# Twenty of the 22 up tiles of a transformer block's second FFN by Strassen's seven products, on one core of a Trainium2 chip

## The chip, the cores and the metric

The kernel runs as one program on one core of a Trainium2 chip. The metric is the device time of one execution in microseconds (us); several runs are compared by their median. A profiled execution gives the trace that all views below are read from.

The engines are named as in the profile: PE is TensorE's matmuls and PEld its weight loads, DVE is VectorE, ACT is ScalarE, POOL is GpSimd, SP is SyncE, whose queue issues transfers here. Each engine works through its own queue in order and waits on semaphores for the others.

## What is computed

Two layers on a sequence of 512 tokens of width 1024, with a context of 256 tokens: the first mixes by a Fourier and a Hyena branch, the second by multi-head latent attention, and each is followed by an FFN with a convolution over the tokens in its gate. The change is in the FFN of the second layer, which works on the 512 tokens alone:

```python
def _conv_ffn(h, w_up, conv_w, conv_b, w_down):
    gate, val = jnp.split(h @ w_up, 2, axis=-1)
    return (jax.nn.silu(_dwconv3(gate, conv_w, conv_b)) * val) @ w_down

def _dwconv3(x, w, b):
    xp = jnp.pad(x, ((0, 0), (1, 1), (0, 0)))
    return xp[:, :-2] * w[0] + xp[:, 1:-1] * w[1] + xp[:, 2:] * w[2] + b

# in reference(), per layer:
    x = x + g2 * _conv_ffn(_modulate(_rms_norm(x, norm2[i]), sh2, sc2), *ffn)
```

All arrays are float32. `w_up` is 1024 x 5632 (gate and value, 2816 each), `w_down` 2816 x 1024.

## The kernel before

Everything stands transposed: 128 features on the partitions, tokens along the free axis, so `x`, and the normalized input `h`, are 8 tiles of 128 x 512. A float32 product is made of three fast matmuls: each operand is split into a rounded high part (`hi`, an ACT copy) and the rest (`lo`, a DVE subtraction), and `mm3` adds high x high, high x low and low x high in PSUM. The three matmuls are lines 158, 159 and 160; the splits are lines 133 and 138, and the loads of raw weights line 146, in the profile.

The hidden width of 2816 is 22 tiles of 128 (`f`). `up(f)` loads two weight tiles of 128 x 1024 (gate and value), splits them, and multiplies each with the 8 tiles of `h` (`hh`, `hl`): 8 k x 2 x 3 = 48 matmuls of 512 columns, or twice as many of 256 for the first tile, which runs by token halves. The gate is convolved (`conv3`: ACT line 373, DVE lines 374 and 375), passed through Silu (line 1175), multiplied with the value (line 1177), and split for the next product. After 8, 16 and all 22 tiles `res_proj` multiplies them by `w_down` for each of 8 output tiles `m`, and line 1143 adds the result, times a gate, to `x`. The down part has 8 x 22 x 3 = 528 matmuls of 512 columns.

PSUM has three buffers of 1024 columns (`mm`) and two of 512 (`ms`); raw, high and low weights have three buffers each (`wr`, `wh`, `wl`, in pool `W`). Raw weights come on SP's queue in the order of their use, as buffers come free. In this part the order of work on the engines is left to the scheduler; in the mixer and the filter (`MIX_ORDER`, `FILTER_ORDER`) and in the attention (`ORDER`) it is written out by hand as a list of steps.

The second layer's `layer1` runs the attention, then the output projection `w_o` by token halves (256-column matmuls), with the norm of the FFN's input hooked in: per half, the squares are summed, `fin` makes the root, and `apply` makes `hh` and `hl` (lines 308, 309, 313). Then it calls `self.ffn(1, ...)`, and `build` writes `x` out.

## Time and profile before

| | |
|---|---|
| median of 3 runs | 1634.23 us |
| lowest, highest | 1628.58, 1636.04 us |
| profiled execution | span 1633.7 us, from its first to its last instruction |
| busy in the span: PE, DVE, ACT, POOL | 1590.5, 1047.7, 620.7, 109.5 us |
| transfers | 173.35 MB, mean 106 GB/s, all issued by SP but for 1.3 MB of instructions |

No other time is recorded for the profiled execution than its span. In the rows of the profile, `L158 PE MATMUL mm<-hh,wh 128*128 128x512` means line 158, the engine, the operation, the tile written and the tiles read, and the shape; then come the count, and behind a bar the busy time, the mean ns of one, and the idle time just before, with what ended it. A row of the timeline begins with the start and the duration in us; a row of the chain of waits gives start, time on the chain, and the step. Matmuls are pipelined, so their durations overlap, and their pace is read from start to start.

### The profile page before, as it was taken

How to read it: one execution, taken by the hardware profiler on the slowest of the kernel's cores; microseconds unless marked ns; L12 is line 12 of the kernel's file. 1: busy time of each engine (PE TensorE's matmuls, PEld its weight loads, DVE VectorE, ACT ScalarE, POOL GpSimd, SP SyncE). 2: the span in 40 equal slices, each digit the busy share in tenths (PEclk: the TensorE clock that was granted, in tenths of full speed). 3: DMA queues.
4: the chain of work that ended last, by engine and by line, in shares of the span. 5: the costliest groups of instructions: out<-in, count | busy, mean ns of one | idle time of the engine just before them, and what ended most of it. 6: DMA issues, size and time to landing. Idle time of an engine off the chain costs nothing.

```text
span 1633.7 us, 20802 instructions
## 1 busy us (share of the span) xinstructions
PE 1590.5 (97%) x8248; PEld 1300.4 (80%) x8248; DVE 1047.7 (64%) x1702; ACT 620.7 (38%) x883; POOL 109.5 (7%) x165
## 2 busy tenths in 40 slices
PE   7999998999999999999999989999999999999999
PEld 5787888888888888888888877666659888878887
DVE  6779869878785355643454665899987544344243
ACT  4441234333222113221033335988954432233131
POOL 0121134000000000000000000212210000000000
PEclk9999998999999999999999998999999999999999
DMA  9336402533443234432342220000024222232222
GB/s 361 109 105 231 156 29 78 192 118 112 159 155 117 77 129 145 164 104 77 113 160 86 83 70 1 13 11 14 0 99 147 78 103 92 90 104 90 90 91 90
DMA packets 54541, 173.35 MB, mean 106 GB/s; under 512 B 6187, under 2 KB 9453, under 8 KB 53421
## 3 DMA queue, kind: packets, MB, share of 16 engines
q1 hardware_dynamic: 54445, 172.03, 30.5%
q8 instruction: 65, 1.06, 0.2%
q14 instruction: 31, 0.25, 0.0%
HBM read 166.24 MB, written 5.77 MB: 105 GB/s over the span
## 4 chain that ended last, share of the span: by engine, by line
PE 81%; DVE 14%; issue 2%; ACT 1%; POOL 1%; DMA 1%; SPq 0%; POOLq 0%; DVEq 0%; ACTq 0%
PE mm L158 24%; PE mm L159 23%; PE mm L160 23%; PE pv L1611 2%; DVE wl L138 1%; DVE S L1587 1%; DVE junk L243 1%; PE s L1557 1%; DVE wr L1626 1%; PE k L158 1%; PE k L160 1%; PE k L159 1%; DVE hl L313 1%; PE mm L616 1%; DVE mx L1571 0%
## 5 line engine op out<-in xcount | busy, mean ns | idle before, releaser
L158 PE MATMUL mm<-hh,wh 128*128 128x512 f32 (+2 forms) x1360 | 481.7, 357 | 1.8 <-ACT wh L133 0.9
L159 PE MATMUL mm<-hl,wh 128*128 128x512 f32 (+2 forms) x1360 | 479.3, 353 | 2.3 <-DVE hl L313 2.3
L160 PE MATMUL mm<-hh,wl 128*128 128x512 f32 (+2 forms) x1360 | 478.7, 353 | 1.6 <-DVE wl L138 1.6
L133 ACT ACTIVATE wh<-wr 128x1024 fp32r<-128x1024 f32 (+1 forms) x192 | 197.8, 1033 | 571.1 <-PE mm L159 547.9
L138 DVE TENSOR_TENSOR wl<-wr,wh 128x1024 fp32r<-128x1024 f32 (+2 forms) x192 | 231.0, 1205 | 236.2 <-ACT wh L133 229.6
L158 PEld LDWEIGHTS mm<-hh,wh 128*128 128x128 f32 x1360 | 257.5, 190 | 48.7 <-issue 7.8
L159 PEld LDWEIGHTS mm<-hl,wh 128*128 128x128 f32 x1360 | 257.8, 190 | 39.0 <-DVE hl L313 3.5
L160 PEld LDWEIGHTS mm<-hh,wl 128*128 128x128 f32 x1360 | 257.6, 190 | 37.6 <-DVE wl L138 2.2
L243 DVE SCALAR_TENSOR_TENSOR junk<-wr,sb 128x1024 bf16<-128x1024 f32 x128 | 156.2, 1220 | 40.4 <-DMA wr<-wmodT 39.8
L158 PE MATMUL mm<-ah,wh 128*128 128x512 f32 (+1 forms) x480 | 172.4, 359 | 0.0
L160 PE MATMUL mm<-ah,wl 128*128 128x512 f32 (+1 forms) x480 | 172.2, 359 | 0.0
L159 PE MATMUL mm<-al,wh 128*128 128x512 f32 (+1 forms) x480 | 172.0, 359 | 0.0
L1143 DVE SCALAR_TENSOR_TENSOR xr<-mm,mod,xr 128x512 f32<-128x512 f32 (+1 forms) x100 | 61.7, 631 | 154.8 <-PE mm L160 153.1
L159 PEld LDWEIGHTS mm<-al,wh 128*128 128x128 f32 x480 | 90.5, 189 | 14.1 <-DVE al L138 0.2
L158 PEld LDWEIGHTS mm<-ah,wh 128*128 128x128 f32 x480 | 90.4, 188 | 14.2 <-issue 0.3
L160 PEld LDWEIGHTS mm<-ah,wl 128*128 128x128 f32 x480 | 90.4, 188 | 14.2
L1611 PE MATMUL pv<-S,V 128*128 128x512 f32 x192 | 93.9, 598 | 2.5 <-ACT S L1590 2.5
L1175 ACT ACTIVATE fg<-fg 128x772 f32<-128x772 f32 (+1 forms) x44 | 32.6, 741 | 97.7 <-DVE fg L375 90.9
L1565 ACT ACTIVATE S<-s,rks 128x512 f32<-128x512 f32 x96 | 62.6, 685 | 12.4 <-PE pv L1611 8.5
L1611 PEld LDWEIGHTS pv<-S,V 128*128 128x128 f32 x192 | 34.5, 190 | 34.7 <-issue 29.3
L1587 DVE TENSOR_TENSOR S<-S,mx 128x1536 f32<-128x1536 f32 x32 | 55.3, 1749 | 2.3 <-POOL mx L1583 2.3
L1583 POOL PARTITION_ALL_REDUCE mx<-mx x16 | 44.9, 2804 | 163.6 <-DVE mx L1580 163.6
(337 smaller groups left out, 2269.6 us busy)
## 6 DMA issues: line engine op xcount, KB each, us to landing
wr<-w_up SPq DMA_DIRECT2D x88, 512.0 KB, 3.2
wr<-wmodT SPq DMA_DIRECT2D x80, 512.0 KB, 3.2
wr<-w_dn SPq DMA_DIRECT2D x32, 512.0 KB, 3.3
wm<-wmod0a SPq DMA_DIRECT2D x8, 1024.0 KB, 9.2
wr<-w_in SPq DMA_DIRECT2D x16, 512.0 KB, 4.2
wr<-w_out SPq DMA_DIRECT2D x13, 512.0 KB, 3.3
wr<-w_dn SPq DMA_DIRECT2D x17, 384.0 KB, 3.0
wr<-w_o SPq DMA_DIRECT2D x11, 512.0 KB, 3.2
```

What stands on the lines that cost most here:

```text
L133: self.nc.scalar.activation(dst, src, AF.Copy)
L138: (eng or self.nc.vector).tensor_tensor(dst, src, hi.bitcast(F32), op=ALU.subtract)
L158: mmul(out, wh, xh, start=start, stop=False)
L159: mmul(out, wh, xl, start=False, stop=False)
L160: mmul(out, wl, xh, start=False, stop=stop)
L243: nc.vector.scalar_tensor_tensor(junk, raw, 1.0, self.sb[:, j, :], op0=ALU.mult, op1=ALU.mult, accum_out=acc)
L1143: nc.vector.scalar_tensor_tensor(x[m][:, a2:b2], ps[:, a2:b2], mod[:, 8 * sec + m, c : c + 1], x[m][:, a2:b2], op0=ALU.mult, op1=ALU.add)
L1175: nc.scalar.activation(g[:, :n], g[:, :n], AF.Silu)
L1565: nc.scalar.activation(c.S[a][j // 3][:, j % 3, :], c.ps[a, j], AF.Copy, scale=c.r[:, g : g + 1])
L1583: nc.gpsimd.partition_all_reduce(c.m[a][:, 1, :], c.m[a][:, 0, :], P, bass.bass_isa.ReduceOp.max)
L1587: v.tensor_tensor(c.S[a][h], c.S[a][h], mb.to_broadcast([P, 3, T]), op=ALU.subtract)
L1611: nc.tensor.matmul(c.P[a], V[:, j, o : o + 128], c.S[a][j // 3][:, j % 3, :], start=j == 0, stop=j == 5)
```

## The change

The second FFN gets its own function, `ffn_blocks`, with its order written out in `UP_ORDER`. Tiles 0 and 1 are made as before (step `U` for tile 1). For tiles 2 to 21 the product of the two weight tiles (gate and value, each with the two halves of the 1024 inputs) with `h` (two halves of the inputs by two halves of the tokens) is a 2 x 2 block product, and is made of seven block products, `P1` to `P7`, of 12 matmuls of 256 columns each:

- The four sums of blocks of `h` are formed once (`T`, in the `quarter` tiles) and split (`Th`, `Tl`). For that `norm` keeps its unrounded result (`whole`), with a further ACT pass.
- The four sums of weight blocks are formed per tile: two by transfers on POOL's queue, the second of each pair adding to what the first has landed (`S1`), two by DVE (`S2`, `S4`). `Hv`, `Hg`, `Ha`, `Hb` and `Lv`, `Lg`, `La`, `Lb` split the value's weights, half of the gate's, and the two tiles of sums. Only half of the gate's raw weights is loaded on SP (`Rg`), all of the value's (`Rv`).
- The blocks of the gate and the value are put together from PSUM by `K1` (ACT) and `C1`, `Ua`, `Xv`, `Ub`, `C2`, `C4`, `C3` (DVE). `Ca`, `Cb`, `Cc`, `Si`, `Ml`, `Ah`, `Al` are the convolution, Silu, the product and its split, as before.

The downs run in five groups of 5, 5, 4, 4 and 4 tiles (`UP_GROUPS`) instead of three, between the ups; `Rd`, `Hd`, `Ld` load and split their weights, `D` multiplies, `X` adds to `x`: 40 of each. In a step's name the numbers are the tile, or the group and the output tile. A list's order holds for PE, DVE, ACT, SP and POOL.

```diff
--- before.py
+++ after.py
@@ -81,6 +81,44 @@
+UP_ORDER = """
+S1.2 Rv2 Rv3 Rg2 S1.3 Hv2 S2.2 T1 Ha2 U1 Lv2 Ca0 Th1 La2 Hg2 Tl1 T3 S4.2 Th3 T2 Rv4 Hb2 Cb0 Th2 Tl3 Lb2 Tl2 S1.4 Cc0 P1.2 Ca1 T4 Si0 P2.2 Lg2 Th4 Ml0
+K1.2 S2.3 P5.2 Ah0 C1.2 Hv3 Tl4 P6.2 Lv3 P7.2 Ha3 Ua2 S4.3 Xv2 P1.3 Rg3 Ub2 La3 P4.2 Rv5 K1.3 C2.2 Cb1 P3.2 S2.4 Hg3 Cc1 Lg3 P2.3 Si1 C3.2 Hb3 Ml1 P5.3
...
+Lb5 Hv6 Hg5 P6.5 C1.5 S1.7 Ca4 Lv6 P7.5 Lg5 Ua5 S2.6 P1.6 Ub5 Ha6 Xv5 C2.5 P4.5 Ml3 K1.6 La6 Ah3 P3.5 S4.6 Cb4 Rg6 P2.6 Hb6 C3.5 Cc4 S2.7 Rd0.0 P5.6
+Si4 Lb6 Hv7 P6.6 Hg6 C1.6 S1.8 Lv7 P7.6 Ha7 Lg6 Ua6 C4.5 P1.7 Ub6 Xv6 C2.6 P4.6 La7 K1.7 Ml4 P3.6 S4.7 Ah4 Al3 Rg7 P2.7 Al4 Hb7 C4.6 C3.6 Rd0.1 Ca5
+P5.7 Lb7 Hd0.0 Hg7 C1.7 P6.7 S1.9 Ca6 Ld0.0 Lg7 Rd0.2 P7.7 Cb5 Hd0.1 Rv8 Ua7 Cc5 D0.0 Ub7 Si5 Xv7 C2.7 Ld0.1 S2.8 Rd0.3 Ml5 P4.7 S4.8 Ah5 X0.0 Cb6 P3.7
...
+Si21 X3.5 Hd4.0 Ml21 Ld4.0 Ah21 Rd4.3 Al21 D3.7 Hd4.1 X3.6 Ld4.1 Rd4.4 D4.0 Hd4.2 X3.7 Ld4.2 Rd4.5 D4.1 Hd4.3 X4.0 Ld4.3 Rd4.6 D4.2 Hd4.4 X4.1 Ld4.4
+Rd4.7 D4.3 Hd4.5 X4.2 Ld4.5 D4.4 Hd4.6 X4.3 Ld4.6 D4.5 Hd4.7 X4.4 Ld4.7 D4.6 X4.5 D4.7 X4.6 X4.7
+"""
+UP_GROUPS = ((0, 5), (5, 10), (10, 14), (14, 18), (18, 22))
+UP_WHOLE = 2
@@ -251,7 +289,7 @@
             self.nc.vector.scalar_tensor_tensor(self.A[i][k][:, j, a:b], sc, 1.0, self.pcol[:, o + a : o + b], op0=ALU.add, op1=ALU.mult)
 
 
-    def norm(self, i, k, x, hh, hl, c0, n, tp):
+    def norm(self, i, k, x, hh, hl, c0, n, tp, whole=None):
 
 
 
@@ -304,11 +342,18 @@
 
         def scaled(d):
             A, B = self.A[i][k][:, j, :], self.mod[i][:, 24 * k : 24 * k + 8, j]
+            if whole is not None:
+                u = box[d] = whole(d)
+                nc.vector.scalar_tensor_tensor(u, x[d][:, c0 : c0 + n], A[:, d : d + 1], box["R"][:, :n], op0=ALU.mult, op1=ALU.mult)
+                nc.scalar.activation(u, u, AF.Identity, bias=B[:, d : d + 1])
+                return nc.scalar.activation(hh[d][:, c0 : c0 + n], u, AF.Copy)
             u = box[d] = tp()
             nc.vector.scalar_tensor_tensor(u[:, :n], x[d][:, c0 : c0 + n], A[:, d : d + 1], box["R"][:, :n], op0=ALU.mult, op1=ALU.mult)
             return nc.scalar.activation(hh[d][:, c0 : c0 + n], u[:, :n], AF.Identity, bias=B[:, d : d + 1])
 
         def low(d):
+            if whole is not None:
+                return nc.vector.tensor_tensor(hl[d][:, c0 : c0 + n], box.pop(d), hh[d][:, c0 : c0 + n].bitcast(F32), op=ALU.subtract)
             B = self.mod[i][:, 24 * k : 24 * k + 8, j]
             return nc.vector.scalar_tensor_tensor(hl[d][:, c0 : c0 + n], box.pop(d)[:, :n], B[:, d : d + 1], hh[d][:, c0 : c0 + n].bitcast(F32),
                                                   op0=ALU.add, op1=ALU.subtract)
@@ -1715,7 +1760,7 @@
         nt = self.pool("nt", bufs=5)
         hp = self.pool("h2p")
         self.xp = self.pool("xres")
-        tp = lambda: self.t(nt, [P, 512], F32, "nt")
+        tp = lambda: self.t(nt, [P, 256], F32, "nt")
         x = [self.t(self.xp, [P, T], F32, f"xr{d}") for d in range(KD)]
         for d in range(KD):
             nc.sync.dma_start(x[d], xd[d])
@@ -1726,14 +1771,302 @@
         half = [[(0, 256)], [(256, 256)]]
         hh = [self.t(hp, [P, T], F32R, f"hh{d}") for d in range(KD)]
         hl = [self.t(hp, [P, T], F32R, f"hl{d}") for d in range(KD)]
-        hook, rest = self.norm_hook(*[self.norm(1, 1, x, hh, hl, c, 256, tp) for c in (0, 256)])
-        self.res_proj(1, 2, oh, ol, KD, lambda m: I["w_o"][m], x, half, hook, ready=2)
-        rest()
+        quarter = [[None] * 2 for _ in range(2)]
+        for a, b in ((0, 0), (0, 1), (1, 1), (1, 0)):
+            quarter[a][b] = self.t(self.xp, [P, 4, 256], F32, "quarter", 5)
+        whole = lambda b: lambda d: quarter[d // 4][b][:, d % 4, :]
+        hook, rest = self.norm_hook(*[self.norm(1, 1, x, hh, hl, 256 * b, 256, tp, whole(b)) for b in range(2)])
+        first = []
+
+        def whook(stage, j, m):
+            hook(stage, j, m)
+            if stage and j == 6:
+                first.extend(self.wload(I["w_up"][1, 0, q]) for q in range(2))
+
+        self.res_proj(1, 2, oh, ol, KD, lambda m: I["w_o"][m], x, half, whook, ready=2)
         self.close("pO")
         self.close("pa")
         self.dbg("xa1", x)
-        self.ffn(1, x, hh, hl, T, [(0, T)], half, None)
+        self.ffn_blocks(x, hh, hl, quarter, first, rest.steps)
         return x
+
+    def ffn_blocks(self, x, hh, hl, quarter, first, steps):
+
+        nc, I = self.nc, self.I
+        v = nc.vector
+        ENG = mybir.EngineType
+        take, f2, a2 = steps
+        i = 1
+        ap = self.pool("act1", bufs=9)
+        tm = self.pool("ftm1", bufs=2)
+        bl = self.pool("blk", bufs=2)
+        th = [self.t(bl, [P, 4, 256], F32R, f"th{q}", 1) for q in range(4)]
+        qf = lambda a, b: quarter[a][b].rearrange("p a b -> p (a b)")
+        tl = [None] * 4
+        form = {"1": (0, 0), "2": (1, 1), "3": (0, 1), "4": (1, 0)}
+        k_ = {}
+        acts = {}
+
+        def T_(n):
+            a, b, c, e = qf(0, 0), qf(0, 1), qf(1, 0), qf(1, 1)
+            if n == "1":
+                v.tensor_tensor(a, a, b, op=ALU.subtract)
+            elif n == "3":
+                v.tensor_tensor(b, e, b, op=ALU.subtract)
+            elif n == "2":
+                v.scalar_tensor_tensor(e, e, -1.0, a, op0=ALU.mult, op1=ALU.subtract)
+            else:
+                v.scalar_tensor_tensor(c, e, -1.0, c, op0=ALU.mult, op1=ALU.subtract)
+
+        def Th(n):
+            self.hi(th[int(n) - 1].rearrange("p a b -> p (a b)"), qf(*form[n]))
+
+        def Tl(n):
+            q = int(n) - 1
+            tl[q] = self.t(self.xp, [P, 4, 256], F32R, "quarter", 5)
+            self.lo(tl[q].rearrange("p a b -> p (a b)"), qf(*form[n]), th[q].rearrange("p a b -> p (a b)"))
+
+        def pair(n=1024):
+            return self.t(self.W, [P, 1024], F32R, "wh")[:, :n], self.t(self.W, [P, 1024], F32R, "wl")[:, :n]
+
+        def Rv(f):
+            k_["rv", f] = self.wraw(I["w_up"][i, f, 1])
+
+        def Rg(f):
+            k_["rg", f] = self.wraw(I["w_up"][i, f, 0]) if f < UP_WHOLE else self.wraw(I["w_up"][i, f, 0, :, 512:1024], 512)
+
+        def H(name, f, src, dst):
+            k_[name, f] = dst
+            self.hi(dst[0], src)
+
+        def L(name, f, src):
+            self.lo(k_[name, f][1], src, k_[name, f][0])
+
+        def Hv(f):
+            H("wv", f, k_["rv", f], pair())
+
+        def Lv(f):
+            L("wv", f, k_["rv", f])
+
+        def Hg(f):
+            if f < UP_WHOLE:
+                k_["wg", f] = [[self.t(ap, [P, T], F32R, f"a{q}") for q in "hl"] for _ in range(2)]
+                for b in range(2):
+                    self.hi(k_["wg", f][b][0], k_["rg", f][:, 512 * b : 512 * b + 512])
+            else:
+                H("wg", f, k_["rg", f][:, 0:512], [self.t(bl, [P, 512], F32R, f"wg{q}", 1) for q in "hl"])
+
+        def Lg(f):
+            if f < UP_WHOLE:
+                for b in range(2):
+                    self.lo(k_["wg", f][b][1], k_["rg", f][:, 512 * b : 512 * b + 512], k_["wg", f][b][0])
+            else:
+                L("wg", f, k_["rg", f][:, 0:512])
+
+        def S1(f):
+            s = k_["sa", f], k_["sb", f] = [self.t(bl, [P, 1024], F32, "sum", 4) for _ in range(2)]
+            g, u = I["w_up"][i, f, 0], I["w_up"][i, f, 1]
+            for t_ in s:
+                nc.gpsimd.dma_start(t_[:, 512:1024], g[:, 0:512])
+            for t_, src in zip(s, (g[:, 512:1024], u[:, 0:512])):
+                nc.gpsimd.dma_start(t_[:, 512:1024], src, accum_op=ALU.add)
+
+        def S2(f):
+            s = k_["sa", f]
+            v.tensor_tensor(s[:, 0:512], s[:, 512:1024], k_["rv", f][:, 0:512], op=ALU.add)
+
+        def S4(f):
+            v.tensor_tensor(k_["sb", f][:, 0:512], k_["sa", f][:, 0:512], k_["rv", f][:, 512:1024], op=ALU.add)
+
+        def Ha(f):
+            H("wa", f, k_["sa", f], pair())
+
+        def La(f):
+            L("wa", f, k_["sa", f])
+
+        def Hb(f):
+            H("wb", f, k_["sb", f], pair())
+
+        def Lb(f):
+            L("wb", f, k_["sb", f])
+
+        def prod(ps, w, o, mov):
+            for q in range(4):
+                s = slice(o + 128 * q, o + 128 * q + 128)
+                self.mm3(ps, w[0][:, s], w[1][:, s], *mov(q), q == 0, q == 3)
+
+        part = lambda a, b: lambda q: (hh[4 * a + q][:, 256 * b : 256 * b + 256], hl[4 * a + q][:, 256 * b : 256 * b + 256])
+        tf = lambda n: lambda q: (th[n - 1][:, q, :], tl[n - 1][:, q, :])
+
+        def P1(f):
+            m = k_["m", f] = self.mm()
+            prod(m[:, 0:256], k_["wv", f], 0, part(0, 0))
+
+        def P2(f):
+            prod(k_["m", f][:, 512:768], k_["wv", f], 512, part(1, 0))
+
+        def P5(f):
+            b = k_["b", f] = self.ms()
+            prod(b[:, 0:256], k_["wa", f], 512, tf(1))
+
+        def P6(f):
+            prod(k_["m", f][:, 0:256], k_["wa", f], 0, tf(2))
+
+        def P7(f):
+            prod(k_["m", f][:, 512:768], k_["wb", f], 512, tf(3))
+
+        def P4(f):
+            prod(k_["m", f][:, 0:256], k_["wg", f], 0, tf(4))
+
+        def P3(f):
+            prod(k_["b", f][:, 0:256], k_["wb", f], 0, part(1, 1))
+
+        def K1(f):
+            k_["t", f] = self.t(bl, [P, 3, 256], F32, "t")
+            nc.scalar.copy(k_["t", f][:, 0, :], k_["m", f][:, 0:256])
+
+        def plus(out, a, b):
+            v.tensor_tensor(out, a, b, op=ALU.add)
+
+        def minus(out, a, b):
+            v.scalar_tensor_tensor(out, a, -1.0, b, op0=ALU.mult, op1=ALU.subtract)
+
+        def C1(f):
+            k_["v", f] = self.t(tm, [P, T], F32, "fv", 3)
+            plus(k_["v", f][:, 0:256], k_["t", f][:, 0, :], k_["m", f][:, 512:768])
+
+        def Ua(f):
+            plus(k_["t", f][:, 1, :], k_["t", f][:, 0, :], k_["m", f][:, 0:256])
+
+        def Ub(f):
+            plus(k_["t", f][:, 2, :], k_["t", f][:, 1, :], k_["m", f][:, 512:768])
+
+        def Xv(f):
+            plus(k_["v", f][:, 256:512], k_["t", f][:, 1, :], k_["b", f][:, 0:256])
+
+        def C2(f):
+            k_["g", f] = self.t(tm, [P, T], F32, "fg")
+            minus(k_["g", f][:, 256:512], k_["t", f][:, 2, :], k_["b", f][:, 0:256])
+
+        def C4(f):
+            minus(k_["g", f][:, 0:256], k_["t", f][:, 2, :], k_["m", f][:, 0:256])
+
+        def C3(f):
+            plus(k_["v", f][:, 256:512], k_["v", f][:, 256:512], k_["b", f][:, 0:256])
+
...
...
+        def Rd(g, m):
+            f0, f1 = UP_GROUPS[g]
+            n = 128 * (f1 - f0)
+            src, o = (I["w_dn"][i, f0 // 8, m], f0 % 8) if f0 // 8 == (f1 - 1) // 8 and f0 < 16 else (None, 0)
+            if f0 >= 16:
+                k_["rd", g, m] = self.wraw(I["w_dn2"][i, m, :, 128 * (f0 - 16) : 128 * (f1 - 16)], n)
...
+        def Hd(g, m):
+            n = 128 * (UP_GROUPS[g][1] - UP_GROUPS[g][0])
+            H("wd", (g, m), k_["rd", g, m][:, :n], pair(n))
+
+        def Ld(g, m):
+            n = 128 * (UP_GROUPS[g][1] - UP_GROUPS[g][0])
+            L("wd", (g, m), k_["rd", g, m][:, :n])
+
+        def D(g, m):
+            ps = k_["d", g, m] = self.mm()
+            h, l = k_["wd", (g, m)]
+            f0, f1 = UP_GROUPS[g]
+            for k in range(f1 - f0):
+                w = slice(128 * k, 128 * k + 128)
+                self.mm3(ps[:, 0:T], h[:, w], l[:, w], acts[f0 + k][0], acts[f0 + k][1], k == 0, k == f1 - f0 - 1)
+
+        def X(g, m):
+            v.scalar_tensor_tensor(x[m], k_["d", g, m][:, 0:T], self.mod[i][:, 40 + m, 0:1], x[m], op0=ALU.mult, op1=ALU.add)
+
...
+        with self.tc.manual_schedule(engines={ENG.PE, ENG.DVE, ENG.Activation, ENG.SP, ENG.Pool}):
+            k_["wg", 0], k_["wv", 0] = first
+            take(KD)
+            Rv(1)
+            Rg(1)
+            Hv(1)
+            Hg(1)
+            U_(0, [(0, 256)], (0, 1))
+            f2(False, 0)
+            U_(0, [(0, 256)], (2, 3, 4, 5))
+            Lv(1)
+            Lg(1)
+            f2(False, 1)
+            U_(0, [(0, 256)], (6, 7))
+            for d in range(KD + 1):
+                if d < KD:
+                    a2(d, 0)
+                if d:
+                    a2(d - 1, 1)
+            U_(0, [(256, 256)], range(KD))
+            for s in UP_ORDER.split():
+                step(s)
+        for n in ("blk", "ftm1", "act1"):
+            self.close(n)
 
     def build(self):
         nc = self.nc
```

77 lines of the change are left out of this document (added).

## The prediction

> **What bounds the kernel now.** I read the page first, then the windows of the last 400 us, the chain of waits there, and the timeline at the second FFN's two ends.
>
> ```profile
> span 1633.7 us, 20802 instructions
> PE 1590.5 (97%) x8248; PEld 1300.4 (80%) x8248; DVE 1047.7 (64%) x1702; ACT 620.7 (38%) x883; POOL 109.5 (7%) x165
> ```
>
> ```profile
> core 0: us, PE busy (x) PEld busy (x) DVE busy (x) ACT busy (x) POOL busy (x), PEclk, DMA share, GB/s
> 1300.00:1400.00 100.00, 100.00 (x431) 80.64 (x431) 43.51 (x50) 31.11 (x38) 0.00 (x0) 1.00 0.28 96
> 1400.00:1500.00 100.00, 100.00 (x432) 80.47 (x431) 42.06 (x49) 32.38 (x40) 0.00 (x0) 1.00 0.27 90
> 1500.00:1600.00 100.00, 100.00 (x435) 81.09 (x434) 41.22 (x48) 27.46 (x34) 0.00 (x0) 1.00 0.28 93
> ```
>
> Columns are the stretch, its length and each engine's busy us with its count of instructions. The page says that a busy PE need not be at its peak, but a count settles it: in the second FFN some 432 matmuls start in 100 us, one every 0.231 us, at full clock (1.00), while DVE is busy 42 us, ACT 31 and POOL none. TensorE sets this stage alone. The chain agrees: from the first matmul to the last sum it is matmul after matmul.
>
> ```profile
> 1255.93 0.28 PE L158 MATMUL mm<-hh,wh 128*128 128x256 f32 x1
> ```
>
> ```profile
> 1322.39 0.38 PE mm L158
> 1355.87 0.39 PE mm L158
> 1629.87 0.75 DVE xr L1143
> ```
>
> The stage lasts from 1255.93 to 1629.87, 374 us, and three up tiles take 1355.87 - 1322.39 = 33.48, so 11.16 us each. An up tile is 48 matmuls of 512 columns (8 k, gate and value, 3 split products).
>
> **The matmuls that go.** Strassen's seven products need, per tile, 7 x 4 x 3 = 84 matmuls, of 256 columns. The projection before the FFN runs that shape:
>
> ```profile
> 1248.18 0.28 PE L158 MATMUL mm<-Oh,wh 128*128 128x256 f32 x1
> 1250.29 0.28 PE L158 MATMUL mm<-Oh,wh 128*128 128x256 f32 x1
> ```
>
> There are 18 starts between these two, 0.117 us each; I take 0.118. So a tile costs 84 x 0.118 = 9.91 us instead of 11.16: two 256-column matmuls (0.236) are dearer than one of 512 (0.2325), or it would be a full eighth. Gain 1.25 us a tile, 25.0 us over 20 tiles. The downs keep their 528 matmuls of 512 columns (regrouped in 5, 5, 4, 4, 4 tiles), tiles 0 and 1 theirs. TensorE's need falls from 374 to 349 us. This is the whole gain; everything else can only give it back.
>
> **What comes in on DVE.** Its steps, priced by start-to-start distances of busy stretches:
>
> ```profile
> 1251.52 0.48 DVE L1143 SCALAR_TENSOR_TENSOR xr<-mm,mod,xr 128x256 f32<-128x256 f32 x1
> 1251.92 0.41 DVE L274 TENSOR_TENSOR nt<-nt,nt 128x256 f32<-128x256 f32 x1
> 1252.25 0.47 DVE L308 SCALAR_TENSOR_TENSOR nt<-xr,A,ms 128x256 f32<-128x256 f32 x1
> 1258.85 1.22 DVE L138 TENSOR_TENSOR wl<-wr,wh 128x1024 fp32r<-128x1024 f32 x1
> 1259.98 0.15 DVE L285 TENSOR_SCALAR nrm_s<-ms 128x2 f32<-128x2 f32 x1
> ```
>
> ```profile
> 1597.61 0.75 DVE L374 SCALAR_TENSOR_TENSOR fg<-mm,pcol,fg 128x511 f32<-128x511 f32 x1
> 1598.27 0.95 DVE L138 TENSOR_TENSOR wl<-wr,wh 128x768 fp32r<-128x768 f32 x1
> 1599.13 0.75 DVE L375 SCALAR_TENSOR_TENSOR fg<-mm,pcol,fg 128x511 f32<-128x511 f32 x1
> ```
>
> The second column is the duration, but the next instruction starts about 0.09 us earlier: 256 columns cost 0.40 (scalar_tensor_tensor) and 0.33 (tensor_tensor), 512 cost 0.66 and, between 0.33 and the 0.86 of 768, about 0.60; 1024 cost 1.13. A Strassen tile needs Lv, La, Lb (3 x 1.13), Lg, S2, S4, Ml, Al (5 x 0.60), Cb, Cc (2 x 0.66), C1, Ua, Ub, Xv, C3 (5 x 0.33) and C2, C4 (2 x 0.40): 10.2 us, against 2 x 1.13 + 2 x 0.60 + 2 x 0.66 = 4.8 before. So **in a tile without downs DVE needs more (10.2) than TensorE (9.9)**. The list holds six such tiles (2 to 7) before the first down, with the four T sums and four Tl of about 1.13 each: 61 + 9 = 70 us of DVE against 11.2 (U1) + 59.5 = 71 of TensorE; the list puts off some convolutions to even it. Two engines full at once, each in a fixed order, wait for each other: P7 needs C1 and Lb, P4 needs Ua, two products (2.8 us) behind. The mixer, also a written order, shows the price:
>
> ```profile
> 250.00:300.00 50.00, 46.69 (x341) 44.65 (x340) 47.62 (x90) 23.32 (x43) 13.06 (x19) 0.93 0.21 74
> ```
>
> There, with DVE busy 47.6 of 50, TensorE idles 3.3 us and loses another 3.5 by its clock (0.93): 14%. That would be 10 us of the 70; the other end is nothing, since tile 0 and 1's convolutions are movable. I take +6. From the first down on, D gives TensorE 123 us in which DVE has only 40 x 0.66 (X) and 40 Ld of 0.60 to 0.73, 53 in all: DVE falls to 75% and no longer bounds. ACT is covered throughout:
>
> ```profile
> L133 ACT ACTIVATE wh<-wr 128x1024 fp32r<-128x1024 f32 x70 | 73.8, 1056 | 170.2 <-PE mm L159 164.5 <-DMA wr<-w_o 2.2 <-issue 2.1
> L373 ACT ACTIVATE fg<-mm,pcol 128x512 f32<-128x512 f32 x22 | 16.8, 762 | 0.0
> ```
>
> After the bar stand busy us and the mean ns of one: three H of 1.06 and five steps (Hg, K1, Ca, Si, Ah) of at most 0.76 make 7.0 us of 9.9.
>
> **The sums by DMA.** S1 puts four transfers of 256 KB on POOL's queue: the gate's half into both sums, then, waiting for each to land, the adding ones. Nothing else stands on that queue. But they start only when Lb two tiles earlier has freed the buffer, and S2 waits for them on DVE, with Lg, La, Lb and C1 queued behind it and P5 and P7 waiting for those. No transfer from POOL is in this trace; the nearest are SP's:
>
> ```profile
> wr<-w_up SPq DMA_DIRECT2D x88, 512.0 KB, 3.2
> xr<-xd SPq DMA_DIRECT2D x8, 256.0 KB, 5.3
> out_dram<-xr SPq DMA_DIRECT2D x8, 256.0 KB, 2.0
> ```
>
> Last column: us from issue to landing. Two in a row cost 4 us at the least (2 x 2.0) and 11 in a queue (2 x 5.3). The list's room, from Lb to the S2 two tiles on, counted in products and downs between them, is 8.5 us (six products of 1.41) for tiles 7, 12, 16, 20, 9.1 for tile 11, 11 to 13 for tiles 4 to 6, over 15 for the rest. At 11 us that costs 4 x 2.5 + 1.9 = 12; at 8 nothing. I take 9, above two of 3.2 (the row for 512 KB, issued with little else) because adding and sharing can only lengthen it: 4 x 0.5, and 1 for what it pushes, +3.
>
> The Trainium skill (DMA: Bandwidth & Descriptors, Anatomy of one DMA) puts a POOL transfer at about 2.0 us plus bytes over 436 GB/s. By that estimate two of 256 KB take 5.2 us, the sums are never late, and the sum would come out 3 us lower; the 2.0 us row agrees with its size, and no run here yet shows an adding transfer.
>
> The raw loads get tight too: Rv19 (512 KB, 3.2 us by its row) is first read 2.8 us of downs after the Ld that frees its buffer, and 17 other loads have 2.8 to 4.2 us. They meet more traffic: 1.75 MB a tile where 1 MB was, beside 11.5 MB of downs as before, about 140 GB/s where the windows show 93, without the adding transfers' second reading. Bounds: 0, where DVE's later room takes it, to 18 x 0.5 = 9. I take +3.
>
> **The start.** norm keeps u whole: one more ACT pass per slice of 256 columns, 16 of 0.40 us by the first row. The start now costs a wait and a spell of slow clock:
>
> ```profile
> 1254.83 0.40 ACT L267 ACTIVATE nt<-xr 128x256 f32<-128x256 f32 x1
> 1258.19 0.38 PE L160 MATMUL mm<-hh,wl 128*128 128x256 f32 x1 [1.63 <-DVE wl L138]
> 1260.27 0.42 PE L159 MATMUL mm<-hl,wh 128*128 128x256 f32 x1
> 1260.48 0.42 PE L160 MATMUL mm<-hh,wl 128*128 128x256 f32 x1
> ```
>
> After 1.63 us of waiting, 256 columns take 0.21. Loading and splitting tile 0 earlier can save that wait and the clock (-4); sixteen passes on the path would be +6. I take 0. The end stays: the last X, then the output.
>
> **Sum.** -25.0 + 6 + 3 + 3 + 0 = -13. Against the profiled span (1633.7 us; the output's landing is inside it) that is 1620.7. The median of the runs is 1634.2, 0.5 above the span: **1621 us**. With all four terms at their low end it would be 1634.2 - 25 - 4 = 1605, with all at the high end 1634.2 - 25 + 37 = 1646; they will not all lie at one end, and the forecast's own range is 1608 to 1626. About 0.5%, 8 us, is what a measurement here can tell from no change.
>
> **Rivals.** *The sums come late.* One mechanism, S2's wait: the adding transfer reads its target as well as its source and POOL prepares each one in turn, so the two steps may take well over 11 us. For it: the room is 8.5 us in five places and the 5.3 us row shows 256 KB can take that long in a queue. Against: DMA is at 0.27 share. At 16 us the waits are 4 x 7.5 + 6.9 (tiles 7, 11, 12, 16, 20) + 4.7 + 3.3 + 3.3 (tiles 4 to 6) + 0.6 (19) = 49: 1634.2 - 25 + 9 + 49 = 1667, slower. It turns the sign when the waits pass 16 us, at a chain of about 12 us. Chance 0.2.
>
> *POOL's work slows DVE.* The attention shows it:
>
> ```profile
> 1173.14 2.61 POOL L1583 PARTITION_ALL_REDUCE mx<-mx  x1 [15.53 <-DVE mx L1580]
> 1174.15 1.41 DVE L1574 TENSOR_TENSOR mx<-mx,S 128x512 f32<-128x512 f32 x1
> 1187.09 0.69 DVE L1574 TENSOR_TENSOR mx<-mx,S 128x512 f32<-128x512 f32 x1
> ```
>
> The same step takes 1.41 beside a POOL instruction and 0.69 without. If each of S1's four preparations did this once, DVE pays 4 x 0.72 = 2.9 us a tile; in tiles 2 to 7 that is 17 us on the path, later DVE's free quarter takes it; and preparations that wait for DVE in turn put S1's chain at its 11 us bound, 9 above the 3 taken: 1621 + 17 + 9 = 1647. Chance 0.1. The skill (SBUF — State Buffer, Who interferes with whom) says that a VectorE step with two SBUF inputs contends with a GpSimd one that reads SBUF, not with one that only writes; by that rule, with descriptors written only, this costs nothing; no run here shows POOL preparing a transfer.
>
> *The order loses more everywhere.* If the mixer's 14% held for all 198 us of Strassen tiles, 28 us are given back, and with 3 for the loads it is 1634 - 25 + 31 = 1640. Against: DVE is full only before the first down, and at 75% after it. Chance 0.15, spread from 1626 to 1645. *It doesn't do what it says*: the built order has the 84 short matmuls per tile, 80 POOL transfers and no full tiles past 1; I give this nothing.
>
> **Chances.** Forecast 0.55. Faster by over 0.5% (below 1626): 0.55. Within: 0.13 of the third rival. Slower: 0.32, the first (0.2), the second (0.1) and the third's far end. The range leaves out the late sums beyond their 16 us case (0.12) and an order without any wait (0.05): 1608 to 1670.
>
> **What would show it.** Right: Strassen products 1.41 us apart, tiles with P only about 9.9 to 10.5 us; DVE near full until the first down and about three quarters later; S2 idle for DMA under 2 us, and at tiles 7, 11, 12, 16, 20 only; stage length near 361 us. Wrong: DVE waits for `sum` at most tiles, or POOL's transfers landing over 6 us after issue (first rival); tensor_tensor of 512 columns well over 0.7 us beside POOL (second); a granted clock under 0.95 past the first down (third).

## The result, and the profile after

The changed kernel takes 1655.6 us (median of 4 runs, 1651.9 to 1662.8) where the kernel before, run beside it, takes 1633.0 us (1628.6 to 1636.0): a ratio of 1.0141, with a 95% interval of 1.0113 to 1.0168. It is slower; the forecast was 1621 us, faster, with the range reaching to 1670.

The page of the kernel after, its span and its engines' busy time, and then three windows of its second FFN (columns as in the windows of before):

```profile
span 1650.0 us, 22867 instructions
PE 1576.6 (96%) x8968; PEld 1319.7 (80%) x8968; DVE 1174.0 (71%) x1963; ACT 670.9 (41%) x980; POOL 166.3 (10%) x245
```

```profile
1300.00:1400.00 100.00, 91.67 (x675) 85.80 (x674) 82.94 (x135) 45.49 (x65) 19.34 (x27) 0.98 0.57 141
1400.00:1500.00 100.00, 94.75 (x631) 85.33 (x630) 73.66 (x116) 39.69 (x55) 15.80 (x22) 1.00 0.56 142
1500.00:1600.00 100.00, 92.16 (x632) 83.11 (x631) 76.44 (x126) 41.56 (x60) 13.84 (x19) 1.00 0.49 124
```

TensorE was busy 100 us of every 100 before; now it is short of that by 5 to 8, in each window, late ones as much as early ones. The clock can't be more than a small part of it: 0.98 in the first window, 1.00 in the others.

Three marks divide the end of the kernel: the first matmul of the output projection's second half, the first whole-width matmul behind tile 0's last one (whole width, 512 columns, is tile 1's), and the last matmul. First before, then after:

```profile
1237.91 0.28 PE L158 MATMUL mm<-Oh,wh 128*128 128x256 f32 x1
1274.30 0.40 PE L159 MATMUL mm<-hl,wh 128*128 128x512 f32 x1
1629.44 0.39 PE L160 MATMUL mm<-ah,wl 128*128 128x512 f32 x1
```

```profile
1240.21 0.28 PE L196 MATMUL mm<-Oh,wh 128*128 128x256 f32 x1
1280.64 0.40 PE L196 MATMUL mm<-hh,ah 128*128 128x512 f32 x1
1645.56 0.40 PE L198 MATMUL mm<-ah,wl 128*128 128x512 f32 x1
```

What lies between the first two is called the start below, between the last two the stage. By these rows they are 36.4 and 355.1 us before. But the scheduler of before had put four of tile 1's whole-width matmuls in between tile 0's, ahead of the mark, here the second of them:

```profile
1270.29 0.40 PE L159 MATMUL mm<-hl,wh 128*128 128x512 f32 x1
```

The four take 0.9 us, so like for like the start is 35.5 us before and the stage 356.1. The start went from 35.5 to 40.4 us, the stage from 356.1 to 364.9. With 2.3 us ahead of the first mark that is 16.0 of the 16.3 us by which the spans differ. The 2.3 us are not the change's: in the traces of the eleven kernels run below, which do the same up to there, this mark lies anywhere from 1236.3 to 1244.6. The same two lengths are given for every experiment, as they leave that spread out.

Who is waited for in the stage after (us in total, times, the longest). The kernel before has no such wait between 1274 and 1630.

```profile
PE mm L196 <- DVE fv L1929: 12.4, 12, 3.4
PE mm L196 <- DVE t L1929: 5.2, 9, 1.0
PE mm L196 <- ACT wh L171: 5.0, 7, 1.3
PE mm L198 <- DVE wl L176: 2.5, 6, 0.5
```

Line 1929 is DVE's putting together of the blocks (C1, Ua, Ub): 21 times TensorE waits for it, 17.6 us in all. (The longest, 3.4 us, is P6 of tile 2 and has another cause, told at e2.) Of the time lost another 7.5 us are waits for split weights. How one of the first kind arises is seen at tile 4, in the timeline of TensorE and then of DVE (a bracket holds the idle time before an instruction and what ended it):

```profile
1319.97 0.28 PE L198 MATMUL mm<-hh,wl 128*128 128x256 f32 x1
1322.79 0.28 PE L198 MATMUL mm<-th,wl 128*128 128x256 f32 x1
1323.67 0.35 PE L196 MATMUL mm<-th,wh 128*128 128x256 f32 x1 [0.60 <-DVE fv L1929]
1326.36 0.28 PE L198 MATMUL mm<-hh,wl 128*128 128x256 f32 x1
1327.05 0.39 PE L196 MATMUL mm<-th,wgh 128*128 128x256 f32 x1 [0.42 <-DVE t L1929]
```

```profile
1323.11 0.42 DVE L1929 TENSOR_TENSOR fv<-t,mm 128x256 f32<-128x256 f32 x1 [1.04 <-PE mm L198]
1325.31 0.42 DVE L1929 TENSOR_TENSOR t<-t,mm 128x256 f32<-128x256 f32 x1 [0.65 <-PE mm L198]
1326.59 0.41 DVE L1929 TENSOR_TENSOR t<-t,mm 128x256 f32<-128x256 f32 x1
```

C1 (1323.11) adds what P2 left in columns 512 to 768. P2's last matmul, the first row, was over at 1320.25, but DVE, idle for 1.04 us, starts only when P6's last (1322.79 + 0.28) is over, which writes columns 0 to 256. P7, which will overwrite P2's columns, must wait for C1 and starts 0.76 us late (1322.79 + 0.12 = 1322.91). P4, which overwrites columns 0 to 256, is released not by Ua (1325.31), their last reader, but by Ub (1326.59), which reads the other half: 0.57 us late. Together 1.33 us, against a gain of 1.25 us that Strassen's products bring per tile.

### The profile page after: what moved, and what is told of

It is laid out like the page before. It is cut to its first block, busy times and chain, and to the rows that moved or that the text cites. A ratio compares the mean times of both kernels' runs of the same rounds, so it can differ in the third digit from the quotient of the medians.

```text
span 1650.0 us, 22867 instructions
## 1 busy us (share of the span) xinstructions
PE 1576.6 (96%) x8968; PEld 1319.7 (80%) x8968; DVE 1174.0 (71%) x1963; ACT 670.9 (41%) x980; POOL 166.3 (10%) x245
## 5 line engine op out<-in xcount | busy, mean ns | idle before, releaser
L196 PE MATMUL mm<-hh,wh 128*128 128x512 f32 (+2 forms) x1192 | 395.2, 333 | 2.7 <-ACT hh L349 1.4
L197 PE MATMUL mm<-hl,wh 128*128 128x512 f32 (+2 forms) x1192 | 394.4, 331 | 2.5 <-DVE hl L358 2.3
L198 PE MATMUL mm<-hh,wl 128*128 128x512 f32 (+2 forms) x1192 | 393.2, 330 | 0.3 <-DVE wl L176 0.3
L171 ACT ACTIVATE wh<-wr 128x1024 fp32r<-128x1024 f32 (+3 forms) x187 | 177.7, 957 | 425.5 <-PE mm L197 391.5
L176 DVE TENSOR_TENSOR wl<-wr,wh 128x1024 fp32r<-128x1024 f32 (+3 forms) x187 | 207.2, 1113 | 119.7 <-ACT wh L171 119.2
L196 PEld LDWEIGHTS mm<-hh,wh 128*128 128x128 f32 x1192 | 224.7, 189 | 31.9 <-issue 2.9
L197 PEld LDWEIGHTS mm<-hl,wh 128*128 128x128 f32 x1192 | 224.5, 188 | 27.5 <-DVE hl L358 3.3
L198 PEld LDWEIGHTS mm<-hh,wl 128*128 128x128 f32 x1192 | 224.6, 188 | 22.5 <-DVE wl L176 0.9
L1188 DVE SCALAR_TENSOR_TENSOR xr<-mm,mod,xr 128x512 f32<-128x512 f32 (+1 forms) x76 | 43.7, 594 | 90.6 <-PE mm L198 89.0
L196 PE MATMUL mm<-th,wh 128*128 128x256 f32 x160 | 47.0, 294 | 13.7 <-DVE fv L1929 12.4
```

Source lines behind the costliest of these rows:

```text
L171: self.nc.scalar.activation(dst, src, AF.Copy)
L176: (eng or self.nc.vector).tensor_tensor(dst, src, hi.bitcast(F32), op=ALU.subtract)
L196: mmul(out, wh, xh, start=start, stop=False)
L197: mmul(out, wh, xl, start=False, stop=False)
L198: mmul(out, wl, xh, start=False, stop=stop)
L1188: nc.vector.scalar_tensor_tensor(x[m][:, a2:b2], ps[:, a2:b2], mod[:, 8 * sec + m, c : c + 1], x[m][:, a2:b2], op0=ALU.mult, op1=ALU.add)
```

## The experiments

Theories. **A**: a wait for a PSUM buffer of 1024 columns counts for both its halves, so that each half's reader waits for the other half's writer and the reverse; against it **A2**, that the same columns' overwriting is waited for. **B**: VectorE has too much to do. **C**: raw weights land late, because POOL's transfers delay them; **C2**, a part of it: DVE stands still for them in its order, and the work queued behind is late. **D**: the start is stretched by the added ACT pass, or by the early loads (**D2**). The lengths of all runs, and the ratio to the kernel before. A length is that of one profiled execution, which was the slowest of twelve for e2 (1636.2 us) and the fastest of twelve for e4 (1632.5 us). A ratio is of medians, to the kernel before run beside it, whose median lay between 1633.0 and 1635.1 us; so times of different rows compare to some 2 us only; the ratios allow for that.

| | start, us | stage, us | ratio, 95% interval |
|---|---|---|---|
| before, like for like | 35.5 | 356.1 | 1 |
| after | 40.4 | 364.9 | 1.0141 (1.0113 to 1.0168) |
| e1 own columns | 40.2 | 365.8 | 1.0138 (1.0118 to 1.0157) |
| e2 split buffers | 41.2 | 344.2 | 0.9969 (0.9954 to 0.9983) |
| e3 no shift pass | 39.3 | 363.6 | 1.0107 (1.0086 to 1.0129) |
| e4 no DVE sums | 40.3 | 346.1 | 1.0029 (1.0017 to 1.0041) |
| e5 split, first weights late | 36.4 | 341.7 | 0.9921 (0.9903 to 0.9939) |
| e6 split, no adding transfers | 41.5 | 330.7 | 0.9869 (0.9856 to 0.9883) |
| e7 split, sums later | 41.5 | 331.6 | 0.9896 (0.9881 to 0.9911) |
| e8 split, no DVE sums | 40.5 | 330.5 | 0.9881 (0.9867 to 0.9896) |
| e9 combined | 36.4 | 331.6 | 0.9883 (0.9866 to 0.9900) |
| e10 combined, no adding transfers | 37.9 | 328.3 | 0.9854 (0.9830 to 0.9878) |
| e11 after, sums later | 41.4 | 354.4 | 1.0045 (1.0033 to 1.0058) |

**e1, own columns in the same buffer.**

```diff
-            prod(k_["m", f][:, 0:256], k_["wa", f], 0, tf(2))
+            prod(k_["m", f][:, 256:512], k_["wa", f], 0, tf(2))
-            prod(k_["m", f][:, 512:768], k_["wb", f], 512, tf(3))
+            prod(k_["m", f][:, 768:1024], k_["wb", f], 512, tf(3))
```

(Ua and Ub read the new columns.)

> P6 and P7 get columns of their own in the same PSUM buffer (256:512 and 768:1024); no instruction is added or moved. In the changed kernel P7 starts late (6.2 us over the twenty tiles) and so does P4 (8.0 us). Theory A, a wait holds for the whole two-bank buffer, whichever columns are read or written: nothing changes, 1653 to 1658 us, P7 and P4 as late as before. Theory A2, the overwriting of the same columns is what is waited for: P7 and P4 start with no gap, 14 us less, about 1641. Theory B, VectorE has too much to do: the waits move to other products, under 4 us less.

1655.8 us, a ratio of 1.0138, as the changed kernel. At tile 4 DVE's C1 and then TensorE's P7, now writing to columns that nothing has used:

```profile
1327.55 0.42 DVE L1929 TENSOR_TENSOR fv<-t,mm 128x256 f32<-128x256 f32 x1 [1.04 <-PE mm L198]
1328.12 0.36 PE L196 MATMUL mm<-th,wh 128*128 128x256 f32 x1 [0.61 <-DVE fv L1929]
```

The same 1.04 and 0.61 us. A2 falls: no column is shared here, and it is waited for all the same.

**e2, two buffers of 512 columns instead of one of 1024.**

```diff
-        return self.t(self.ps, [P, 1024], F32, "mm", 3)
+        return self.t(self.ps, [P, getattr(self, "mw", 1024)], F32, "mm", 3)
+    def mv(self):
+        return self.t(self.ps, [P, 512], F32, "mv", 3)
...
-            m = k_["m", f] = self.mm()
+            m, k_["n", f] = self.mm(), self.mv()
+            k_["m", f] = m
...
```

From the output projection on `mw` is 512; P1, P6 and P4 write to `m`, P2 and P7 to `n`, P5 and P3 to `ms` as before ("P3's partners" in the expectation are these two). The total of PSUM and the order of all instructions are the same.

> The two banks of a PSUM buffer become two buffers of 512 columns (three of each): P1, P6, P4 in the one, P2, P7, P3's partners as before in the other; no instruction is added or moved. Theory A, whole-buffer waits: C1 then runs at the end of P2 instead of P6, Ua at the end of P6 instead of P7, and the gaps before P7 (6.2 us), P4 (8.0) and those before P6 that are C1's (about 4 of 10) go: 14 to 18 us less than the changed kernel, 1637 to 1642 us, ratio to the kernel before 1.002 to 1.006. Theory B, VectorE has too much to do: PE waits for the low parts of the weights instead, under 5 us less, over 1650. Theory C, raw weights land late: as B, with DVE idle before the sums.

1629.0 us, 26 us less than the changed kernel where A expected 14 to 18, and below the kernel before; the stage is 20.7 us shorter. At the same place of tile 4 now P6's first matmul, C1 beside it, and P7's first with no wait (TensorE, DVE, TensorE):

```profile
1326.29 0.28 PE L199 MATMUL mm<-th,wh 128*128 128x256 f32 x1
1326.38 0.42 DVE L1934 TENSOR_TENSOR fv<-t,mv 128x256 f32<-128x256 f32 x1
1327.64 0.28 PE L199 MATMUL mv<-th,wh 128*128 128x256 f32 x1
```

The wait for the blocks is gone from the list, but for 0.7 us:

```profile
PE mm L199 <- ACT wh L174: 3.0, 3, 1.6
PE mm L199 <- ACT t L1931: 3.0, 1, 3.0
PE mm L201 <- DVE wl L179: 2.6, 6, 0.5
PE mv L199 <- DVE fv L1934: 0.7, 1, 0.7
```

The row with `ACT t` is P6 of tile 2, which waited 3.4 us in the changed kernel too: there C1 stands between, but what is late is K1, on ACT. Counted by product in the two traces, the waits before P7 fall from 4.8 to 0.7 us, before P4 from 5.2 to 0, and before P6 from 8.8 to 3.0. That is 15.1 of the 20.7 us; most of the rest is matmuls that follow each other faster (last section).

The split also leaves `n` to P2 and P7 alone, since the downs take only `mm`, so these two have more buffers to go round. That is not what helps: in the changed kernel TensorE never waits for a free buffer. P1 and P2, the first to write, wait 0.3 us in all, and that, like every wait of D, is for split weights. Whether the chip or the program sets the grain of these waits, no run here shows.

e2 also decides against B in the opening, the tiles ahead of the first down. The window 1320 to 1340, in tiles 3 to 6, of after and of e2:

```profile
1320.00:1340.00 20.00, 18.20 (x152) 17.49 (x151) 17.42 (x29) 10.06 (x14) 5.22 (x7) 1.00 0.59 136
```

```profile
1320.00:1340.00 20.00, 20.00 (x178) 20.00 (x177) 19.99 (x36) 11.53 (x16) 5.74 (x8) 1.00 0.70 172
```

TensorE is busy 20.00 of 20 us and DVE 19.99: both full, in a written order, and neither loses anything. The Trainium skill (Perfetto Trace Analysis, Matmuls) advises to let independent groups of matmuls rotate through different PSUM banks, so that one is emptied while the next is computed. The products here lay in different halves of the buffer already; e1 and e2 show that it takes buffers that are waited for apart.

**e4 and e8, without DVE's two sums per tile,** in the changed kernel and on top of the split.

```diff
-... Ua4 S2.5 Xv4 P1.5 Ha5 Ub4 ... P3.4 S4.5 Cb3 ...
+... Ua4 Xv4 P1.5 Ha5 Ub4 ... P3.4 Cb3 ...
...
+        sums = [self.t(bl, [P, 1024], F32, f"sum{n}", 1) for n in range(4)]
+        for t_ in sums:
+            nc.gpsimd.memset(t_[:, 0:512], 0.5)
```

Every S2 and S4 leaves the list in the same way.

> The two sums that DVE forms per tile (S2, S4) are left out, so the lower half of the weights' sums holds a constant, and with them DVE's waits for the raw value weights at these two places; 40 DVE steps of 0.69 us, 27 us of DVE time, less. Theory A: the gaps before P7 and P4 stay, only waits for late weights go (P6 and D, about 6 us of them): 1648 to 1653. Theory B, VectorE's throughput sets the tile: 16 to 25 us less, 1630 to 1640. Theory C, the raw weights' lateness: 6 to 12 us less, with DVE's idle time of 17.6 us before the sums gone.

1639.8 us: by its number B's expectation.

> On top of the split buffers: DVE's two sums per tile are left out as before (the lower half of the sums holds a constant), 27 us of DVE work less and no DVE wait for raw weights there. If only the blocked queue costs (theory C2): D's waits go and little else, 8 to 10 us less than with split buffers, 1619 to 1621. If DVE's throughput costs too (theory B): the remaining waits in the opening (P6, P7 and P1, 6 us) go as well, 13 us or more less, under 1616.

1615.3 us, 13.7 less than e2, over C2's 8 to 10 and just past the line that was drawn for B. Neither number alone decides, but e7 does (below): there DVE keeps these 27 us of work, only elsewhere in its order, and the stage is 331.6 us against e8's 330.5. So the work itself is worth 1 us, and what e4 and e8 took away was a wait in the queue. In the changed kernel S2 or S4 also stands between Ua and Ub of tiles 2 to 5, where P4 waits for Ub by theory A, so e4 shortens these waits too.

**e7 and e11, eight pairs of sums later in DVE's order,** on the split, and on the changed kernel alone.

```diff
-... Rv14 C2.13 S2.14 P4.13 X1.4 S4.14 P3.13 C4.13 ... Hd1.7 Ld1.6 Ld1.7 Rv15
+... Rv14 C2.13 P4.13 X1.4 P3.13 C4.13 ... Hd1.7 Ld1.6 Ld1.7 S2.14 S4.14 Rv15
```

> On top of the split buffers: DVE's two sums of tiles 8, 10, 11, 13, 14, 17, 18 and 21 stand in the list behind the low parts of the next down's weights, which DVE now makes first; nothing is added. Theory C2, DVE stands still for raw weights (22.7 us) and the downs' weights queued behind wait with it: D's waits (9.4 us) fall under 3 us, the time by 5 to 8 us, 1621 to 1624, ratio 0.992 to 0.9945. Rival, the sums then come too late for the tile's own high parts on ACT: the waits move to P5 and P6 and the time stays at 1628 to 1632.

1618.3 us, 10.7 less than e2, where C2 expected 5 to 8, and 12.6 us less of stage. What was to go is DVE's first row in e2, its wait for raw weights ahead of S2, and with it D's waits for split weights:

```profile
DVE sum L1880 <- DMA wr<-w_up: 22.7, 9, 6.0
```

In e7 no DVE wait for `wr` is left, and of TensorE's there are two rows:

```profile
PE mm L199 <- ACT t L1931: 3.1, 1, 3.1
PE ms L199 <- DVE fg L1937: 0.7, 2, 0.3
```

> The changed kernel with nothing but the eight pairs of sums later in the list; PSUM buffers as they were. If the waits for whole buffers and the blocked queue cost apart from each other: D's waits (8.8 us) go, those before P7, P4 and P6 stay, 1645 to 1649 us, ratio 1.007 to 1.010. If DVE's idle time at the sums is hidden in the changed kernel behind the waits for whole buffers: within 3 us of 1655.

1641.1 us, better than either expectation, and 10.5 us of stage: the two losses lie apart from each other, 20.7 and 12.6 us one after the other (364.9, 344.2, 331.6), or 10.5 and 22.8 in the other order (364.9, 354.4, 331.6).

**e6, without the adding transfers,** on the split; the sums lack a block.

```diff
-            for t_, src in zip(s, (g[:, 512:1024], u[:, 0:512])):
-                nc.gpsimd.dma_start(t_[:, 512:1024], src, accum_op=ALU.add)
```

> On top of the split buffers: the adding transfers on POOL's queue are left out, 40 of 256 KB, so that the weights' sums lack a block. Theory C, the transfers that POOL adds delay the raw weights: DVE's wait for raw weights before its sums (22.7 us with split buffers) falls under 12 us, the waits of D (9.4 us) with it, and the time falls by 4 to 8 us, 1621 to 1625. Rival, the raw weights are late because their buffers come free late in the written order: the waits stay over 17 us, the time within 2 us of 1629.

1613.4 us, twice what C expected: the raw weights come early enough where they stand. DVE's wait:

```profile
DVE sum L1878 <- DMA wr<-w_up: 7.7, 7, 2.6
```

POOL's queue in e2 and in e6 between 1290 and 1620 (packets, MB, share of the 16 engines):

```profile
q0 software_dynamic: 8064, 18.88, 26.9%
```

```profile
q0 software_dynamic: 2800, 9.18, 8.6%
```

The adding transfers are 9.70 MB of this and 18.3 points, so 1.9 points for a MB, if the plain ones cost the same in both runs; the plain ones take 0.94. Each adding transfer occupies the engines like two. Beside them SP's loads of 512 KB land later, 4.2 us after issue at the median against 3.5:

```profile
wr<-w_up SPq DMA_DIRECT2D x18, 512.0 KB, 4.2
```

```profile
wr<-w_up SPq DMA_DIRECT2D x17, 512.0 KB, 3.5
```

So C and C2 are both true: the transfers delay the raw weights, and the order turned the delay into lost time.

**e3 and e5, the start.** e3 leaves out the added ACT pass, and with it the shift; e5, on the split, loads tile 0's weights after the output projection.

```diff
-                nc.scalar.activation(u, u, AF.Identity, bias=B[:, d : d + 1])
```

> The additional ACT pass of the norm is left out, and with it the addition of the shift to the normalized input: 16 ACT passes of 256 columns less. Theory D, the start is stretched by ACT's queue, in which the weights' high parts stand behind these passes: the second FFN's first product starts 4 to 8 us earlier and the time is 1647 to 1651. Rival, the start is stretched by the two gate tiles loaded early in the output projection: under 2 us less, 1653 to 1656.

1651.4 us; the start is 39.3 us instead of 40.4. The pass costs 1 us of the start, not D's 4 to 8, and the intervals of the two ratios overlap.

```diff
-            if stage and j == 6:
-                first.extend(self.wload(I["w_up"][1, 0, q]) for q in range(2))
...
+        first.extend(self.wload(I["w_up"][1, 0, q]) for q in range(2))
         self.ffn_blocks(x, hh, hl, quarter, first, rest.steps)
```

> On top of the split buffers: the first two weight tiles of the second FFN are loaded and split after the output projection's last weights, not before them; 0 instructions more. Theory D2, the early loads push the last output-projection weights back (its product waits 2.98 and 1.69 us for them in the changed kernel, not at all in the one before): these waits go, the first tile waits some 2.6 us as it did before the change, 2 to 4.5 us less than with split buffers, 1624.5 to 1627, ratio 0.994 to 0.9957. Rival, the stretch comes from the additional ACT pass of the norm alone: no gain, 1628 to 1631.

1621.9 us; the start is 36.4 us, 4.8 us less than e2's, as D2 has it. The 0.9 us that are left over the kernel before fit the ACT pass. (2.5 us of the stage go as well, at the downs' waits for weights, which e5 does not touch: they differ from run to run.) The output projection's last product in the changed kernel, whose weights are loaded and split behind tile 0's by SP, ACT and DVE:

```profile
1258.39 0.39 PE L196 MATMUL mm<-Oh,wh 128*128 128x256 f32 x1 [2.82 <-ACT wh L171]
1260.42 0.58 PE L198 MATMUL mm<-Oh,wl 128*128 128x256 f32 x1 [1.53 <-DVE wl L176]
```

and all that TensorE waits for in e5's start:

```profile
PE mm L201 <- DVE wl L179: 2.1, 1, 2.1
PE mm L199 <- ACT hh L352: 1.4, 1, 1.4
```

**e9, the parts that help together,** with K1 of tile 2 ahead of T4's split in ACT's order; and **e10**, the same without the adding transfers.

> Split buffers, the first weights loaded late, the eight pairs of sums later in the list, and K1 of tile 2 moved ahead of ACT's passes T4 waits for (P6 of tile 2 waits 3.1 us for it with split buffers). If the three losses lie in different places and add up: split buffers with later sums 0.9896 of the time before, 4.8 us of the start less (half of the output projection to the first whole tile: 41.2 to 36.4 us), 3 us of P6 less, that is about 1610 us, ratio 0.984 to 0.987. If they hide one another: 1615 to 1618, ratio 0.988 to 0.9896.

1614.8 us, a ratio of 0.9883: faster than both kernels. But it lies in the range that was expected if the parts hide one another, 4 us short of their sum. Moving K1 gave nothing in the stage (331.6 us as in e7): the 3.1 us before P6 of tile 2 are gone, and P7 behind it waits 2.2.

```profile
PE mm L201 <- DVE wl L179: 2.5, 2, 2.1
PE mv L199 <- DVE fv L1933: 2.2, 1, 2.2
PE mm L199 <- ACT hh L352: 1.4, 1, 1.4
```

The start's 5 us are there in the trace (36.4 against e7's 41.5), but of them the ratios show 2 (0.9896 to 0.9883), with intervals that overlap; where the rest went is open.

> As the combined kernel, without the adding transfers on POOL's queue, so that the weights' sums lack a block. If the transfers' extra load costs only by the raw weights that DVE waits for at a place where other work is queued behind: within 2 us of the combined kernel, since the sums stand later there. If it costs by itself (weights late elsewhere): 4 us or more less.

1611.3 us, 3.5 below e9, with intervals that overlap, between the two expectations; the stage is 3.3 us shorter. The adding transfers may cost some 3 us beyond the blocked queue, which these runs do not settle.

## Why the prediction was wrong, point by point

- **The matmuls that go, -25: right.** With the other losses taken away the stage is 330.5 to 331.6 us (e8, e7), 24.5 to 25.6 us below the 356.1 of before, the opening's wait still in it. The gain is all there, a part of it by a pace that was faster than priced (last section); that this just makes up for the opening's wait is luck.
- **A step that was missing: the products' hand-over through PSUM, 20.7 us (after to e2).** The prediction wrote that P7 needs C1 and P4 needs Ua, "two products (2.8 us) behind", and took DVE's load for what decides whether they come in time. That is the order by columns. As built, the other half of the buffer comes between: Ua waits for P7, and P4 for Ub. Of C1 and P6, the one that stands later in the list waits for the other: in eight tiles, as in tile 4, C1 waits for P6 and P7 for C1, with no product between; in the other twelve P6 waits for C1, with P5 alone between. So one product, or one D, at most lies between hand-over and reuse where two were counted. This is the step that failed, and it is enough by itself to turn the sign: 1621 + 20.7 is 1642, slower. With this alone mended the kernel is faster than before (e2, 0.9969); with the other large loss mended and not this one it is still slower (e11, 1.0045).
- **The opening, +6: the size was about right by luck, the reason not.** Two full engines were to cost up to 14% as in the mixer; in e2 they cost nothing over 20 us. What the opening does cost without the buffer waits is a single place: P6 of tile 2 waits 3.0 us for K1, queued on ACT behind a step that waits for T4, and the products just behind it run slow, 5.6 us in all from P5 to the next tile's P1. Why the mixer loses 14% no run here looked for.
- **"DVE falls to 75% and no longer bounds": true, and not enough.** It is busy 74 to 76 us of 100 past the first down, and TensorE loses 5 to 8 us of each 100 there too. What bounds is how long a step takes to come round, not how full its engine is.
- **The sums by transfers, +3: measured 0 in the changed kernel.** DVE waits for `sum` nowhere. (In e7 and e9, which are quicker, it does, 3.0 and 4.5 us in all.) A landing takes 4.2 us at the median, as the page has it (count, KB, us from issue to landing):

```profile
wr<-w_up SPq DMA_DIRECT2D x68, 512.0 KB, 3.5
sum<-w_up POOLq DMA_DIRECT2D x80, 256.0 KB, 4.2
```

  Two in a row are 8.4 us, close to the 9 taken and to the room of 8.5. By the Trainium skill's formula for such a transfer (DMA: Bandwidth & Descriptors, Anatomy of one DMA) the two would take 5.2 us as an estimate; here the trace differs, beside other traffic, and decides.
- **The raw loads, +3 (0 to 9): the mechanism was right, the size far off: 10.5 to 12.6 us of stage (e11, e7).** The bound took 0.5 us for each of 18 loads, as if each were late alone. What was not priced is the queue: in e2 DVE stood up to 6.0 us before one S2 while the next down's weights waited behind it. The adding transfers' second reading was named there and left out of the 140 GB/s; measured, such a transfer takes twice a plain one's share of the engines.
- **The start, 0 (-4 to +6): +4.9 us.** The ACT pass is 1 of it (e3). The early loads, which were to save 4, cost 4.0 to 4.8 (e5's start against the changed kernel's and e2's): the call is placed before the output projection's last load, and the prediction priced a step moved earlier without what it is moved ahead of.
- **The rivals.** Late sums: refuted, as above. POOL's work slowing DVE: refuted, S2 takes what the step took in the attention without POOL. First the minimum, median and maximum of S2 in ns, then POOL's preparing of adding transfers (882 ns each), then an S2 and a preparing that overlap:

```profile
L1876 DVE TENSOR_TENSOR sum<-sum,wr x20: 684/687/694, 1279.8 to 1593.5; 128x512 f32<-128x512 f32 x20
L1872 POOL DMA_DIRECT2D sum<-w_up x36 | 31.8, 882 | 40.8 <-DMA sum<-w_up 35.6 <-issue 3.0 <-DVE fg L1932 2.2
1325.65 0.69 DVE L1876 TENSOR_TENSOR sum<-sum,wr 128x512 f32<-128x512 f32 x1
1326.12 0.86 POOL L1872 DMA_DIRECT2D sum<-w_up  x1 [2.28 <-DMA sum<-w_up]
```

  Four of the 40 S2 and S4 overlap with the preparing of an adding transfer, and take 685 to 686 ns. The Trainium skill's rule (SBUF — State Buffer, Who interferes with whom) is borne out as far as this goes. The third, an order that loses everywhere, came nearest: its 1640 has the right sign and the right place, all tiles, but its cause, a full DVE, is refuted by e2, and its share of 0.15 was too small because the argument against it looked at busy shares.
- **The sum of what was found.** Without both large losses the stage is 24.5 us shorter than before (e7, the opening's wait in it). With 20.7 for the hand-over, 12.6 for the raw loads, 4.9 for the start and 2.3 ahead of it that is 16.0 of the 16.3 us between the two spans. The medians lie 22.6 us apart: the profiled execution of the changed kernel took 1651.9 us, 3.7 less than its median, and what makes its other executions longer was not profiled. That 1655.6 lies within the range as far as 1670 is luck as well: that end was the late sums', and the sums are not late.

## What to carry to other kernels

Before counting how many products lie between a hand-over and its reuse, find out at what grain the waits are kept: here two halves of one PSUM buffer waited for each other, and giving each its own buffer, with no instruction added or moved, was worth 26 us. In an order written by hand, put a step that waits for a transfer behind everything on its engine that others wait for, since it is the queue behind the wait that costs. An engine at 75% can cost as much as a full one, and two full engines can cost nothing.

## What the runs showed of the hardware

An adding transfer from POOL's queue took twice the DMA engines' time of a plain one of its size (1.9 against 0.94 points of share for a MB), and its landing was not the problem. What it did to the others' was: loads of 512 KB on SP's queue landed 4.2 us after issue instead of 3.5, and DVE's wait for them at the sums was 22.7 us instead of 7.7 (e2, e6).

Matmuls of 256 columns ran at two paces at the same granted clock of 1.00. In the changed kernel at tile 4, P2's first and the first of P5, which comes 12 matmuls later:

```profile
1318.67 0.28 PE L196 MATMUL mm<-hh,wh 128*128 128x256 f32 x1
1320.09 0.28 PE L196 MATMUL ms<-th,wh 128*128 128x256 f32 x1
```

That is 0.118 us each, the pace priced. In e2 P2 of the same tile starts here, and P6, 24 matmuls later, at 1326.29 (shown at e2):

```profile
1323.57 0.28 PE L199 MATMUL mv<-hh,wh 128*128 128x256 f32 x1
```

That is 0.113 us each. At 84 matmuls a tile the difference is 0.4 us, 7 to 8 us over twenty tiles if it held throughout. On the whole the kernels with fewer waits ran more of their 140 products at the faster pace (under 0.115 us from start to start): 42 in the changed kernel with 34 waits of TensorE in the stage, 74 in e2 with 11, 64 in e5 with 10, 96 in e7 with 3, 108 in e6 with 1. A wait may so cost more than its own length, but that is not shown, and what sets the pace was not tried.
